# A fused matmul and batch norm on one core: work of VectorE moved to ScalarE and GpSimd, two output blocks turned another way, and the order of all work given as a table

## The chip, the cores and the metric

The kernel runs on one core of a Trainium2 chip. A core has five engines with instruction streams of their own: TensorE (PE) multiplies matrices, VectorE (DVE), ScalarE (ACT) and GpSimd (POOL) work on tiles, and SyncE (SP) issues transfers. Transfers run on 16 DMA engines, which all queues share; "the wire" is short for them. On-chip data lies in SBUF. TensorE writes into PSUM, of which there are eight banks here. The metric is the device time of one execution in microseconds, and the time before is the median of three runs.

## What is computed

```python
batch, m, k, n = 16, 512, 1024, 768
...
y = np.matmul(x, weight)
mean = np.mean(y, axis=(0, 1), keepdims=True)
var = np.var(y, axis=(0, 1), keepdims=True)
y_norm = (y - mean) / np.sqrt(var + eps)
return (gamma * y_norm + beta).astype(np.float32)
```

x is 8192 rows of 1024, the weight 1024 by 768, all float32. Mean and variance are taken per output column over all 8192 rows, so nothing of a column can be written before all its rows are multiplied. Products are made in bfloat16 and accumulated in float32. The output has 25.2 MB.

## The kernel before

**Tiles.** The rows are cut into 16 chunks of 512 (`C`, chunk `c`), the 768 columns into six tiles of 128 (`nt`). x is loaded chunk by chunk on GpSimd's queue until 100 us and turned by VectorE (L435). The first and second tile (`GA = 2`) are multiplied "by rows", x stationary, so that the result stands as it is stored (`rows_unit`, L510); only chunks 14 and 15 of them are multiplied "by columns" (`ga_unit`, L814) and turned later (`ga_block`). The third to sixth tile (nt 2 to 5) are multiplied "by columns", weight stationary (`col_unit`, L575), in halves of the contraction; a result then lies transposed and must be turned before it is stored. The third, fourth, fifth and sixth tile follow one another on TensorE.

**Statistics.** A result in PSUM is read twice: for its statistics and for a bfloat16 copy into SBUF ("keep"). On VectorE the statistics are one `bn_stats` (L711), with the keep on ScalarE (L715). For the tiles and chunks in `ASTAT` ScalarE does both, a keep with its sum (L720) and a square with its sum (L724); `total` (L978) then puts the sums together before the tile's variance is made. When a tile's chunks are done, variance, root and scale follow (`finish_tasks`).

**Output of the first two tiles** (`rows_out`). A block takes a product with the scale on VectorE (L937), an addition of the shift on GpSimd (L942) or, for the blocks in `ADDED`, on VectorE, and a store. The scale and shift rows are spread over the partitions by TensorE (`spread_rows`, L903); GpSimd has no access to PSUM in this kernel, and its shift row is copied to SBUF first (`shift_sbuf`).

**Output of the others.** A block has two chunks, 1024 rows. There are three ways:
- "pe": a norm (`norm`, L1021) on the columns, eight transposes on TensorE (`turn_block`), a copy from PSUM on ScalarE (L1210), a store (L1202). The eight transposes may ride inside a later matmul unit, one after each matmul ("hosted").
- "xact": the norm, a transpose by DMA on SP's queue (L1220), a conversion to float32 on ScalarE (L1232), a store.
- "raw" (`RAW`): the kept values are turned by DMA before the scale is known (`raw_turn`, L1106). The scale is then spread over rows (`raw_spread`: turn, gather, deal, keep), and the block takes a product on VectorE (L1174), an addition on GpSimd (L1178) and a store (L1182). Five blocks go this way.

**The tail.** The fifth tile's last block is held until the last matmul (`held_block`, L1252). The sixth tile's statistics are only complete then: aggregate, root (L1311), scale (L1324), and for each block norm (L1348), transposes (L1044), copy (L1361), store (L1364).

**Order.** Every step above is a `Task` with the engines that may run it, an estimate of its time, and a due time (`prio`). `arrange` plays the whole kernel through with those estimates. It picks the next task by due time among those that can begin within 0.2 us of the earliest. It also picks the engine where a task has several, places its buffers (PSUM banks through `Pool`, SBUF through `Space`), and decides which transposes ride in which matmul unit. The instructions are then issued to each engine in exactly the order that comes out (`seq`). On the chip an engine runs its own list in order and waits by semaphores for the others.

Of the kernel before, what the change touches and what calls it, by code (L numbers as in the profile page):

```python
# [120 lines left out]

def arrange(tasks, turns, log=None):
# [6 lines left out]
    left = sorted(tasks, key=lambda t: t.prio)  # L129
    order = []  # L130
    SEM, LOOK = 0.06, 0.2
# [36 lines left out]
    while left:  # L168
        seen = [(t, ready(t)) for t in left]
        first = {}  # L170
        for t, r in seen:
            if r is not None:
                for e in t.engines:
                    b = start_of(t, r, e)
                    if e not in first or b < first[e]:
                        first[e] = b
        if not first:
            raise RuntimeError(f"nothing can begin: {[(t.prio, t.emit) for t in left[:8]]}")
        e = min(first, key=lambda k: first[k])
        best = None  # L180
        for t, r in seen:
            if r is not None and e in t.engines and start_of(t, r, e) <= first[e] + max(LOOK, t.look):
                if best is None or t.prio < best[1]:
                    best = start_of(t, r, e), t.prio, t
        start, _, t = best
# [4 lines left out]
        if t.hosts:  # L190
            room = t.hosts
            for u, r in seen:
                if u in turns and r is not None and r <= start + 0.3 and room >= 1:
                    n = min(room, turns[u][0])
                    if turns[u][0] == turns[u][1]:
                        places = [s.pool.place(s) for s in u.takes]
                        if any(p is None or p[0] > start for p in places):
                            continue
                        for s in u.takes:
                            s.pool.take(s, s.pool.place(s)[1])  # L200
                        u.takes_done, u.takes = u.takes, []
                    t.hosted.append((u, n))
                    turns[u][0] -= n
                    room -= n
                    occ += 0.0555 * n
                    lat += 0.0555 * n
# [12 lines left out]
        left.remove(t)  # L219
        for u, n in t.hosted:  # L220
            if turns[u][0] == 0:
                u.end = t.end + 0.2
                left.remove(u)
# [4 lines left out]
def kernel(  # L228
# [136 lines left out]
    def act(occ):  # L365
        return {"ACT": (occ, occ + 0.11)}
# [549 lines left out]

    U = S - 30.0
# [9 lines left out]
    sh = task(U, act(0.3), shift_sbuf, [p1], uses=[a1_slot])  # L927


    def rows_out(c, s0, s1, k):  # L930
# [19 lines left out]
        a = task(due, dve(0.3 * n), norm, [p0] + keeps, takes=[slot], uses=[y_row[c], a0_slot])  # L950
# [5 lines left out]
    k = 0  # L956
# [6 lines left out]
    def negate_gamma(eng):  # L963
        seq(nc.vector.tensor_scalar(ngamma, gamma_sb, -1.0, None, op0=ALU.mult))

    ng = task(S, dve(0.1), negate_gamma, [affine, sr], True)

    def finish_tasks(nt):
# [41 lines left out]
        if nt in ASTAT:  # L1010
            deps = [task(now + 1.0, {"ACT": (1.2, 1.3)}, total, deps)]
# [44 lines left out]
    def ga_block(c, due):  # L1056
# [4 lines left out]
        def norm_ga(a):  # L1061
            def emit(eng):
                part = yslot.y[:, a]
# [348 lines left out]
```

## Time and profile before

| | |
|---|---|
| time, median of 3 runs (lowest to highest) | 206.29 us (206.23 to 206.86) |
| span of the profiled execution | 204.07 us |
| the median less that span | 2.22 us |
| TensorE, VectorE, ScalarE, GpSimd busy | 189.3, 159.3, 146.2, 124.1 us |
| last matmul of the sixth tile ends | 186.62 us |
| read from memory, written | 36.71 MB, 25.17 MB |

The span runs from the first to the last instruction of one execution under the profiler; no total time is known for that execution, so its span is set against the median of the runs. In the slices of the page the span is cut into 40 equal parts and a digit is the busy share in tenths. A line of the chain has a start, a length and the work that the end was waiting for. A line of a stage has the busy time of each engine, with the count of instructions in brackets. A line of waits has who waited for whom, and the total, the count and the longest in microseconds.

### The profile page before, as it was taken

Reading aid. Unit: us, or ns where it says so; the run is one execution under the profiler, and the core shown is the slowest. Engines: PE = TensorE matmul, PEld = TensorE weight load, DVE = VectorE, ACT = ScalarE, POOL = GpSimd, SP = SyncE. Lnnn points to the kernel's source line nnn. Section 1 sums busy time; section 2 is a strip of 40 time slices with the busy share of each in tenths; the row PEclk is TensorE's granted clock in tenths of the full one; section 3 lists DMA queues with packets and bytes.
Section 4 is the critical chain, followed back from the end, with each engine's and each line's share of the span. In section 5 each row is a group of like instructions: output and inputs, shape, how many; then the busy total and the mean of one; then the engine's idle time right before and its main releaser. Section 6 shows DMA issues by size and latency. Waiting matters only on the chain.

```text
span 204.1 us, 3510 instructions
## 1 busy us (share of the span) xinstructions
PE 189.3 (93%) x1210; PEld 114.5 (56%) x1210; DVE 159.3 (78%) x250; ACT 146.2 (72%) x260; POOL 124.1 (61%) x150
## 2 busy tenths in 40 slices
PE   7969999999999999999999999999999999997900
PEld 3457554657488888777865444444444445544600
DVE  4031879999999999969989998987999878657900
ACT  2001461368989999899978766999998959956950
POOL 7776954877499989997403999389613312940000
PEclk9999999999999999999999999999999999999965
DMA  4999999999999999999686899899999999999998
GB/s 71 172 199 196 176 196 196 196 197 197 190 193 197 197 196 196 196 197 195 103 181 200 297 339 336 248 301 328 295 322 227 336 303 274 347 343 310 310 347 253
DMA packets 98562, 48.74 MB, mean 239 GB/s; under 512 B 24304, under 2 KB 98032, under 8 KB 98544
## 3 DMA queue, kind: packets, MB, share of 16 engines
q0 software_dynamic: 34624, 18.36, 65.5%
q1 hardware_dynamic: 63920, 30.16, 52.6%
q8 instruction: 9, 0.15, 0.3%
q14 instruction: 9, 0.07, 0.1%
HBM read 36.71 MB, written 25.17 MB: 303 GB/s over the span
## 4 chain that ended last, share of the span: by engine, by line
PE 86%; ACT 3%; DMA 3%; POOL 2%; issue 1%; ACTq 0%; DVE 0%; POOLq 0%
PE y_ps L575 54%; PE y_ps L510 24%; PE y_ps L814 4%; ACT o_sb L1361 3%; DMA ring<-in_x_dram 3%; PE o_ps L1044 1%; POOL ring L403 1%; POOL w_sb L387 1%; PE y_ps L753 1%; PE a_ps L903 1%; PE o_ps L1074 0%; ACTq L1407 0%; PE idle_ps L591 0%; PE tot_ps L871 0%; ACT ring L1252 0%
## 5 line engine op out<-in xcount | busy, mean ns | idle before, releaser
L575 PEld LDWEIGHTS <-w_sb 128*128 128x128 bf16 x520 | 50.3, 97 | 57.6
L575 PE MATMUL y_ps<-xT_sb,w_sb 128*128 128x512 bf16 (+1 forms) x272 | 59.3, 371 | 0.0
L575 PE MATMUL y_ps<-x_pl,w_sb 128*128 128x512 bf16 x248 | 57.4, 379 | 0.0
L403 POOL DMA_DIRECT2D ring<-in_x_dram x76 | 47.2, 626 | 14.4 <-DMA ring<-in_x_dram 5.5
L510 PE MATMUL y_ps<-w_sb,xT_sb 128*128 128x256 bf16 x448 | 50.6, 273 | 1.7 <-DMA ring<-in_x_dram 1.6
L510 PEld LDWEIGHTS <-xT_sb 128*128 128x128 bf16 x448 | 43.5, 98 | 9.4 <-DVE xT_sb L435 2.9
L435 DVE STREAM_TRANSPOSE xT_sb<-ring 128x1024 f32<-128x1024 f32 (+1 forms) x29 | 31.2, 1111 | 14.1 <-DMA ring<-in_x_dram 13.9
L711 DVE BATCH_NORM_STATS2 stats<-y_ps 128x6 f32<-128x512 f32 x46 | 30.9, 687 | 7.7 <-PE y_ps L575 7.2
L715 ACT CAST y_sb<-y_ps 128x512 bf16<-128x512 f32 x51 | 29.0, 593 | 10.4 <-DVE stats L711 6.3
L547 ACT COPY x_pl<-xT_sb 128x1024 bf16<-128x1024 bf16 x32 | 32.8, 1063 | 1.7 <-DVE xT_sb L435 1.7
L942 POOL TENSOR_TENSOR ring<-ring,sum 128x1024 f32<-128x1024 f32 (+1 forms) x11 | 23.8, 2188 | 14.9 <-ACT y_ps L724 10.9
L659 ACT ACTIVATE sq_sb<-y_ps 128x512 f32<-128x512 f32 x28 | 16.3, 610 | 16.2 <-PE y_ps L510 15.9
L666 POOL TENSOR_TENSOR sum<-sum,sq_sb 128x512 f32<-128x512 f32 x20 | 25.6, 1278 | 3.0 <-ACT sq_sb L659 1.7
L662 DVE TENSOR_TENSOR sum<-y_ps,sum 128x512 f32<-128x512 f32 x28 | 18.9, 675 | 6.3 <-ACT sq_sb L659 5.3
L672 ACT CAST y_sb<-y_ps 128x512 bf16<-128x512 f32 x28 | 16.3, 594 | 8.2 <-DVE sum L662 8.0
L1178 POOL TENSOR_TENSOR ring<-ring,sum 128x1024 f32<-128x1024 f32 x6 | 14.8, 2477 | 9.8 <-issue 8.5
L937 DVE TENSOR_TENSOR ring<-y_sb,a_ps 128x1024 f32<-128x1024 bf16 (+1 forms) x16 | 16.7, 1079 | 0.1
L1044 PE MATMUL o_ps<-ident,y_sb 128*128 128x128 bf16 x104 | 13.1, 221 | 1.6 <-DVE y_sb L1348 1.5
L1232 ACT CAST ring<-ring 128x1024 f32<-128x1024 bf16 x13 | 13.8, 1063 | 0.6 <-DMA ring<-y_sb 0.6
L1145 POOL COPY sum<-sum 32x256 f32<-32x256 f32 (+1 forms) x17 | 5.8, 340 | 13.4 <-DVE sum L1142 6.5
L428 DVE STREAM_TRANSPOSE xT_sb<-ring 128x2048 bf16<-128x2048 bf16 x6 | 13.5, 2290 | 0.1
L591 PE MATMUL idle_ps<-idle_sb 128*128 128x512 f32 x18 | 9.6, 688 | 1.5 <-DVE idle_sb L316 1.5
(104 smaller groups left out, 153.7 us busy)
## 6 DMA issues: line engine op xcount, KB each, us to landing
out_dram<-ring SPq DMA_DIRECT2D x37, 512.0 KB, 3.4
ring<-in_x_dram POOLq DMA_DIRECT2D x52, 256.0 KB, 8.8
out_dram<-o_sb SPq DMA_DIRECT2D x6, 512.0 KB, 4.7
ring<-in_x_dram POOLq DMA_DIRECT2D x16, 128.0 KB, 5.9
w_sb<-in_weight_dram POOLq DMA_DIRECT2D x8, 192.0 KB, 6.2
out_dram<-ring SPq DMA_DIRECT2D x6, 256.0 KB, 3.0
ring<-in_x_dram POOLq DMA_DIRECT2D x4, 192.0 KB, 7.8
out_dram<-o_sb SPq DMA_DIRECT2D x3, 256.0 KB, 2.5
```

The source lines that it names most:

```text
L403: bi = seq(nc.gpsimd.dma_start(x_bf[32 * i:32 * i + 32], src[:, :, KQ * i:KQ * (i + 1)]))
L435: seq(nc.vector.transpose(dst, src[:, :, jw0:jw1]))
L510: seq(nc.tensor.matmul(y_ps[:, s], x_of(c, jw, e, t * P, (t + 1) * P), w_sb[:, jw, e, 0:NA], start=(s == 0 and jw == 0 and e == 0), stop=( ...
L547: seq(nc.scalar.copy(dst, pairs) if eng == "ACT" else ENG[eng].tensor_copy(dst, pairs))
L575: seq(nc.tensor.matmul(y_ps, w_sb[:, jw, e, nt * P:(nt + 1) * P], moving(c, jw, e, q0 * QR, q1 * QR, parted), start=(jw == 0 and e == 0 an ...
L659: seq(nc.scalar.activation(sq_sb[:, 0:n], slot.tile[:, 0:n], AF.Square))
L662: seq(nc.vector.tensor_add(sum1, slot.tile[:, 0:n], sum1))
L666: seq(ENG[eng].tensor_add(acc, acc, state["sq"][:, 0:n]))
L711: seq(nc.vector.bn_stats(dst, slot.tile))
L715: seq(nc.scalar.copy(y(nt, c), slot.tile))
L937: seq(nc.vector.tensor_mul(slot.o, y_row[c].y[:, s0:s1], aff[0][:, None, :].to_broadcast([P, n, NA])))
L942: seq(ENG[eng].tensor_add(slot.o, slot.o, row[:, None, :].to_broadcast([P, n, NA])))
```

## The change

1. `ORDER`, a table of 785 words, replaces the choice in `arrange`. A word is an engine's letter (P TensorE, V VectorE, A ScalarE, G GpSimd, S SP) and a task's number in order of creation; behind a plus sign stand the transposes that ride along, as block and count. `arrange` still places the buffers and plays the times through, in the table's order.
2. `RAW` of the fourth tile becomes `(0, 2)`: its block of chunks 2 and 3 goes the raw way, as the sixth raw block. It went the "xact" way.
3. `MODE` of the fifth tile: the block of chunks 8 and 9 goes the "xact" way. It went the "pe" way.
4. `ASTAT` gets the fourth tile's chunks 12 and 13. Their statistics are made on ScalarE, and `total` is done for that tile too; it now waits only for the chunks that it sums.
5. `SCALED = (2,)`: the product of the second half of chunk 0 in `rows_out` moves to GpSimd, which reads the scale row from a copy in SBUF that ScalarE makes (`scale_sbuf`).
6. `negate_gamma` moves from VectorE to GpSimd and doesn't wait for the first tiles' shift any more.
7. `norm_ga` of chunk 15 may run on ScalarE; in the table one of its two halves does.
8. `PAD` goes from 50 to 28. The tile `stats` gets 528 bytes shorter per partition; the two new tiles of `ASTAT` take 128 and 400.

Up to the end of x's loads, about 97 us, the table has the order of the kernel before on every engine. Behind that it differs on all of them. Some words of it: S664 is the DMA transpose of the fifth tile's chunks 8 and 9 and S575 that of the fourth tile's last block; P660, P668 and P672 are transposes of the fifth tile's blocks; P536 is the first half of the fourth tile's chunk 11 and A507 the keep of its chunk 15; A457 makes the third tile's scale; A727 is the last root, A733 and A736 the copies of the held block; V750, P751, A752 and S753 are norm, transposes, copy and store of the sixth tile's chunk 2, 512 rows. The fifth tile's "gather" is G647, on GpSimd; it ran on ScalarE.

```diff
+ORDER = (
+    "G0 P59 G3 G8 A9 G4 G7 V1 V2 P60 G10 P61 P62 P63 P64 P65 V5 V6 P66 G12 P67 P68 P69 P70 P71 G14 P76 A72 "
...
+    "V329 P421 P425 P330 P331 P422 A318 A332 A333 A389 V384 V334 V383 V335 V388 P385 P426 P390 A386 S393 S398 "
...
+    "S366 S369 V456 V371 V526 V373 V510 V502 A457 A468 A488 A472 A476 A494 S469 S372 S473 A503 A470 P504 P517 "
+    "P505 P496 V379 V506 V458 V518 A511 A480 A507 A474 A527 A484 A519 A495 G377 G374 G380 G459 G460 S378 S471 "
+    "S375 P610 P520 P536 P497 P537 P512 P513 P532 P533 P521 S477 S481 S381 S475 A498 A461 A478 V579 V580 V581 "
...
+    "A572 V645 V671 V659 V667 V677 V663 V685 V646 V681 A686 A641 A678 G647 P695+668.3 P691+660.4 P699+660.4 "
+    "P687 P688 P692+672.1,668.1 P700+668.1,672.1 P696+668.3,672.1 S569 S664 S575 G648 A661 A665 A682 A649 "
+    "A576 V693 V689 V650 V701 G651 A694 A669 A702 A690 S573 S662 S666 S577 P711+672.1 P707+672.3 P708 P712 "
+    "P719 P703+672.1 P704 P715 P716 V653 V656 V713 V697 V720 V709 V731 V705 V725 A673 A710 A714 A706 A698 "
+    "G654 G729 G657 P722 V717 V723 P735 P732 V726 V728 A718 A721 A727 A733 S670 S652 S655 S674 S658 V730 V750 "
+    "V754 V738 V746 V755 P751 P739 P747 A736 A724 A752 A740 A748 V742 V759 V780 V769 V784 V760 V774 V764 V770 "
...
+)
...
-    left = sorted(tasks, key=lambda t: t.prio)
+    left = tasks
...
+    NAMES = {"P": "PE", "V": "DVE", "A": "ACT", "G": "POOL", "S": "SP"}
+    for word in ORDER.split():
+        word, _, riders = word.partition("+")
+        t, e = left[int(word[1:])], NAMES[word[0]]
+        r = ready(t)
+        if r is None:
+            raise RuntimeError(f"out of order: {word}")
+        start = start_of(t, r, e)
...
-    PAD = 50
+    PAD = 28
...
-    ASTAT = {2:tuple(range(4,16))}
+    ASTAT = {2:tuple(range(4,16)),3:(12, 13)}
...
-    ADDED = (0,6,16,28,40)
+    ADDED, SCALED = (0,6,16,28,40), (2,)
...
-    MODE = {2:'xact',3:'xact',4:('pe',)*8}
+    MODE = {2:'xact',3:'xact',4:('pe','pe','pe','pe','xact','pe','pe','pe')}
...
-    RAW, RAWADD, RAWDUE = {2:(0,2),3:(0,),4:(0,2,4)}, {2:'POOL',3:'POOL',4:'POOL'}, {2:14.0,3:8.0,4:8.0}
+    RAW, RAWADD, RAWDUE = {2:(0, 2),3:(0, 2),4:(0, 2, 4)}, {2:'POOL',3:'POOL',4:'POOL'}, {2:14.0,3:8.0,4:8.0}
...
+    def scale_sbuf(eng):
+        seq(nc.scalar.copy(sum3[:, NA:2 * NA], aff[0]))
...
-            seq(nc.vector.tensor_mul(
-                slot.o, y_row[c].y[:, s0:s1], aff[0][:, None, :].to_broadcast([P, n, NA])))
+            row = sum3[:, NA:2 * NA] if eng == "POOL" else aff[0]
+            seq(ENG[eng].tensor_mul(slot.o, y_row[c].y[:, s0:s1], row[:, None, :].to_broadcast([P, n, NA])))
...
+        on = pool(0.59 * n) if k in SCALED else dve(0.3 * n)
...
-        seq(nc.vector.tensor_scalar(ngamma, gamma_sb, -1.0, None, op0=ALU.mult))
-
-    ng = task(S, dve(0.1), negate_gamma, [affine, sr], True)
+        seq(nc.gpsimd.tensor_scalar(ngamma, gamma_sb, -1.0, None, op0=ALU.mult))
+
+    ng = task(S, pool(0.3), negate_gamma, [affine])
...
-            deps = [task(now + 1.0, {"ACT": (1.2, 1.3)}, total, deps)]
+            deps = deps + [task(now + 1.0, {"ACT": (1.2, 1.3)}, total, [col_end[nt, c][0] for c in ASTAT[nt]])]
...
+                if eng == "ACT":
+                    seq(nc.scalar.activation(
+                        part, part, AF.Identity, bias=shift[:, a:a + 1], scale=scale[:, a:a + 1]))
+                    return
...
-        norms = [task(due, dve(0.25), norm_ga(a), [sr] + [h[1] for k, h in ga_half.items() if k[1] == c], True, uses=[yslot])
+        norms = [task(due, dve(0.25) if c == RC else {**dve(0.25), **act(0.48)}, norm_ga(a), [sr] + [h[1] for k, h in ga_half.items() if k[1] == c], True, uses=[yslot])
...
```

More of the change, by code (lines that the diff above doesn't have):

```diff
@@ L166, in start_of @@
         return b
[L168 to L185, printed above, removed]
+    NAMES = {"P": "PE", "V": "DVE", "A": "ACT", "G": "POOL", "S": "SP"}
[6 more added lines that the diff above has]
+        start = start_of(t, r, e)
         for s in t.takes:
@@ L189, in arrange @@
         t.hosted = []
[L190 to L206, printed above, removed]
+        for rider in riders.split(",") if riders else ():
+            i, n = rider.split(".")
+            u, n = left[int(i)], int(n)
+            if turns[u][0] == turns[u][1]:
+                for s in u.takes:
+                    s.pool.take(s, s.pool.place(s)[1])
+                u.takes_done, u.takes = u.takes, []
+            t.hosted.append((u, n))
+            turns[u][0] -= n
+            occ += 0.0555 * n
+            lat += 0.0555 * n
         if t in turns:
@@ L218, in arrange @@
         order.append(t)
-        left.remove(t)
         for u, n in t.hosted:
@@ L927 @@
     sh = task(U, act(0.3), shift_sbuf, [p1], uses=[a1_slot])
+    sh0 = task(U, act(0.3), scale_sbuf, [p0], uses=[a0_slot])
     def rows_out(c, s0, s1, k):
```

6 lines of the change are left out of this document (3 added, 3 removed), and 27 rows, old and new, of the table ORDER.

## The prediction

> **What bounds the kernel now.** I read the page's busy shares and slices first, then the chain that ended last, then the waits of TensorE, then busy time by stage, and last the DMA slices of the final 54 us.
>
> ```profile
> PE 189.3 (93%) x1210; PEld 114.5 (56%) x1210; DVE 159.3 (78%) x250; ACT 146.2 (72%) x260; POOL 124.1 (61%) x150
> PEclk9999999999999999999999999999999999999965
> DMA  4999999999999999999686899899999999999998
> ```
>
> ```profile
> 106.66 1.05 PE a_ps L903 x8
> ...
> 109.95 0.45 PE o_ps L1074 x8
> 110.40 58.94 PE y_ps L575 x269
> 169.34 0.06 PE o_ps L1044
> ...
> 177.82 6.99 PE y_ps L575 x32
> 184.80 1.81 PE y_ps L753 x16
> 186.62 0.24 PE o_ps L1044 x4
> ```
>
> ```profile
> PE o_ps L1044 <- DVE y_sb L1348: 1.5, 1, 1.5
> ```
>
> The chain (start, us, what) is TensorE without a break from 24 us to 186.6. In the list of TensorE's waits nothing lies between the start and the 1.5 us at 187, where the last tile's scale is awaited. The clock is full throughout. So until 186.62 the time is the sum of TensorE's instructions, whatever the other engines do, as long as none makes it wait.
>
> Behind 186.62 come 17.45 us of tail: 2.69 to the issue of the last tile's first store (189.31), then 4.19 MB of stores. The wire in that stretch (GB/s, slices of 1.35 us from 150 on):
>
> ```profile
> GB/s 314 327 326 312 152 131 348 305 346 342 232 329 347 294 318 324 150 347 348 347 347 346 340 342 347 346 346 341 210 293 268 345 346 347 348 346 347 346 331 1
> ```
>
> 346 is its ceiling. It is full from 173 to 188.8, drops to 210, 293, 268 until 192, then is full to the end: 4.19 MB at 346 GB/s are 12.1 us. The dip shows that the older stores have run out before the last tile's arrive. So the end is "last matmul, time to the first store of the last tile, 12.1 us of wire". Busy time by stage, for cover (stage, its length, then PE, PEld, DVE, ACT, POOL with counts, clock, DMA share, GB/s):
>
> ```profile
> 132.00:144.00 12.00, 12.00 (x57) 5.36 (x55) 9.93 (x15) 12.00 (x18) 11.19 (x12) 1.00 1.04 310
> 144.00:156.00 12.00, 12.00 (x58) 5.38 (x56) 11.76 (x27) 11.32 (x18) 4.64 (x8) 1.00 1.19 316
> 180.00:187.00 7.00, 7.00 (x47) 4.01 (x44) 3.93 (x9) 3.14 (x7) 2.05 (x1) 1.00 1.14 343
> ```
>
> ScalarE and VectorE have no room between 132 and 156 and plenty after 180.
>
> **The parts of the change.**
>
> Fifth tile, chunks 8 and 9, turned by DMA. TensorE loses 8 transposes; eight of them standing together took 0.45 us (L1074 above), and each takes 0.06 inside the stream. They lie on the path: **-0.45 us**. The ScalarE copy from PSUM (1.01, L1210) becomes a conversion in SBUF (1.06, L1232): nothing. SP gains one DMA transpose, 1.3 to 2.4 us (L1220).
>
> Sixth raw block (fourth tile, chunks 2 and 3). Its transpose moves from the full stretch near 155 to the five at 100 to 107 us, of 1.25 us each (L1106), where the wire carries nothing else; all six end near 108.3, before the first output store's issue at 109.1. VectorE: 1.21 (L1174) for 0.54 (L1026). ScalarE: no conversion, -1.06. GpSimd: +2.48 (L1178). With the first part, the DMA transposes in the full stretch stay at 14, so the wire's work there changes by 0; at worst +1.28 (one transpose), which the dip of 1.04 us would mostly take up.
>
> Statistics of the fourth tile's chunks 12 and 13 on ScalarE: VectorE -2 x 0.69 (L711); ScalarE's casts of 0.59 become pairs of 1.17 (L720, L724 with their reads, start to start), +1.16, and the summing adds 0.9 (L980 to L986, 123.25 to 124.15) between the last statistic and the root. That wait holds up the conversions and copies behind it on ScalarE, and the fourth tile's stores; not TensorE, unless banks run out (below).
>
> The table moves two of the sixteen re-layout copies (L547) from ScalarE (1.06) to VectorE (0.68), one rows-scaling of 0.68 (L937) from VectorE to GpSimd (at the add's 1.29, L942), one 0.41 (L1064) to ScalarE (between the 0.59 of L715 and half of L1023's 1.25), adds a 0.37 copy for the scale, moves four small copies of the fifth tile (1.0) from ScalarE to GpSimd, and a 0.16 negation likewise. Sums: VectorE -0.68 -0.41 -0.16 -1.38 +0.67 +1.36 = -0.6; ScalarE +0.6 +0.37 +1.16 +0.9 -1.06 -2.12 +0.05 -1.0 = -1.1; GpSimd +1.29 +0.2 +2.48 +0.9 = +4.9 of a span in which it idles 80. All covered by TensorE's stream: 0. Without that cover, VectorE and ScalarE would return 0.6 and 1.1.
>
> One row speaks against leaning on GpSimd: a VectorE copy of L547 at 143.1 took 0.96 where the median is 0.68, and a raw add was running (141.1 to 146.3). The new 4.9 us can meet about as many copies and norms as two raw adds do, at most four: 4 x 0.28 = 1.1 us, covered. The Trainium skill (SBUF — State Buffer, "Who interferes with whom") has a two-port VectorE copy and a GpSimd instruction block each other fully. By that, the sum for VectorE would be four waits of up to a whole raw add; by the row it is four of 0.28, and the trace, with no copy above 0.96, agrees with the page on the contact and not on its size.
>
> The spread of the first tiles' scale. In the table the first and second tile's scale is spread (L903) behind only 4.3 us of other TensorE work after the sums, against 7.1 now. TensorE now idles 0.09, 0.07 and 0.05 there. The chain's last input ends about 0.9 earlier too. I take **-0.1**, between -0.2 (the idle gone) and 0.
>
> Banks. The table leaves half-finished units open and statistics waiting. I walked the tightest place by rows. When chunk 11 of the fourth tile begins, eight PSUM banks are held (chunks 9, 8, 6, 12, 15, 13, 7 and an opened fifth-tile one); it needs chunk 15's. TensorE arrives at 136.8: the third tile ends at 122.8 (the spreads' end, 107.7, plus 15.1 of halves), then 9 halves of 0.86 and 7 of 0.9. ScalarE starts the third tile's scale at 126.45, as now, and has 0.79, five norms of 1.15, one statistic of 0.6, three casts of 0.48 and one conversion of 0.95 before the bank is free: 136.0. Slack some 0.7 us, where the kernel now shows no such wait: **0**, with an open upper end.
>
> Tail. The table puts the root ahead of both held copies (it started 0.04 after its input anyway: 0) and makes a 512-row block the first of the last tile instead of a 256-row one. Its norm costs 0.06 more (0.405 against 0.342), two more transposes 0.11, its copy 0.24 (0.616 against 0.376): the first store goes out 0.41 later. It brings 256 KB instead of 128, so the two gaps of the first small stores close: they are issued 0.47 and 0.51 apart and fill the wire for 0.38 each, 0.22 together. **+0.2**, between -0.2 (the delay hidden behind held stores still on the wire) and +0.4.
>
> Sum: -0.45 -0.1 +0.2 = -0.35. The profiled execution spans 204.07; the median of the runs is 206.29, 2.22 above it, which I keep: 203.72 + 2.22 = **205.9 us**.
>
> **Rivals.**
> - The tail comes out early (faster): TensorE's saving arrives whole, the idle at 106 goes and the first store isn't late. -0.45 -0.2 -0.2: 205.4. For it: the wire dips by 1.04 us there, so anything sooner counts. Against: the larger first block. Chance 0.31.
> - ScalarE late, banks run out (slower). Place: 125 to 137, from the inversion of the third tile's deviation to chunk 15's cast. Now that inversion ends 0.9 us after its root, behind a 1.2 us product. Two norms' worth of lateness, 2.3, less the slack of 0.7, stalls TensorE 1.6: 207.5. It decides from a lateness of 1.7 (a stall of 1.0). Against: no such stall now. Chance 0.22.
> - VectorE blocked outright by GpSimd (slower): two blocks of a whole 2.48 between 132 and 156, where VectorE has 2.3 idle of 24, would leave 2.7 us and stop TensorE for about that: 208.6. The largest seen is 0.28, so 0.06. This is the page's rule named above.
> - The wire sets the end, and TensorE's saving is hidden (no change). The fourth tile's last DMA transpose stands behind the fifth tile's new one on SP, which waits for that tile's scale (166.2 now), three norms and a statistic ahead of its own norm (4 x 0.54 + 0.69) and then takes 1.7: issued near 170.7, two microseconds later than the 168.7 now. If older stores still fill the wire when the first last-tile store comes, the saving is gone: one transpose of 1.28 less the dip of 1.04, 206.5. Chance 0.06. The Trainium skill (Advanced Engine Details and Errata, "X-Bar Transpose (TRN2)") has transposes as fast as ordinary transfers; five of 256 KB in 6.86 us (the timeline, L1106) are 191 GB/s against 346, so the trace disagrees.
>
> **How the numbers follow.** The forecast, 0.35, has its own range from its bounds, 205.4 to 206.2. I call within 0.3% of the median "same" (205.67 to 206.91), about what a measurement can tell. Faster 0.31, from the first rival; same 0.35 + 0.06 = 0.41; slower 0.22 + 0.06 = 0.28. The range 205.2 to 207.6 goes down to the early tail and up to the bank rival, and leaves out the outright block, the longer stalls and a tail better than any row shows.
>
> **What would show it.** Right: TensorE unbroken to 186.0 to 186.2, 24 hosted transposes, six transposes at 100 to 108.3, first last-tile store about 3.1 us after the last matmul, a smaller or equal dip on the wire. Wrong: TensorE waiting on ScalarE or VectorE between 120 and 175 (banks); L547 copies on VectorE near 2 us (outright block); a full wire from 186 to the end (wire). A gain over 1.1 us would mean a saving that I don't see, since nothing else in the chain moves.

## The result and the profile after

The changed kernel takes 209.75 us (median of 6 runs, 208.97 to 210.35). The kernel before, run beside it, takes 206.12 (205.84 to 206.86). The ratio is 1.017, with a 95% interval of 1.0144 to 1.0197: the change costs 3.6 us. I had predicted 205.9 us and a range of 205.2 to 207.6.

The profiled execution took 210.35 us and spans 208.56. First the page of the changed kernel, with its busy shares, the slices of TensorE's clock, and the wire in GB/s (40 slices of 5.2 us):

```profile
PE 190.3 (91%) x1202; PEld 115.4 (55%) x1202; DVE 161.6 (77%) x248; ACT 144.9 (69%) x267; POOL 131.1 (63%) x157
PEclk9999999999999999999999999999999999999695
GB/s 75 159 196 191 169 196 196 196 197 197 190 194 196 197 197 195 196 197 193 99 121 114 381 385 333 279 346 297 317 249 252 264 325 326 348 322 227 313 347 226
```

TensorE's clock is full up to the last matmul, as it was before. Then TensorE's waits in it (who waits for whom; total, times, longest), of which the kernel before had only the load's, the start's and 1.5 us of the last-tile line:

```profile
PE o_ps L1074 <- DVE y_sb L1382: 3.1, 3, 2.7
PE y_ps L534 <- DMA ring<-in_x_dram: 1.7, 1, 1.7
PE idle_ps L615 <- DVE idle_sb L340: 1.5, 1, 1.5
PE o_ps L1108 <- DVE y_sb L1098: 1.3, 1, 1.3
PE y_ps L599 <- ACT y_sb L739: 0.2, 1, 0.2
```

And its chain (start, length, what). Before, it was TensorE without a break from 24 us to 186.6. Now it is on TensorE from 80.9 on, leaves it from 108.7 to 110.8, then from 142.5 to 174.0, where it runs over GpSimd, ScalarE and above all VectorE, and from 183.7 on until the last tile's scale is made. The first and the last of these:

```profile
107.62 1.07 PE a_ps L927 x8
108.99 0.37 ACT sum L942
109.39 0.69 DVE ring L966
110.08 0.68 DVE y_sb L1098
110.80 0.62 PE o_ps L1108 x8
...
181.75 1.96 PE y_ps L599 x9
183.73 1.30 DVE stats L735 x2
...
185.96 2.17 DVE y_sb L1056
188.13 0.61 DVE stats L735
...
190.88 0.32 ACT std L1345
```

Near its end stands a norm of VectorE (L1056) of 2.17 us on the chain, 2.25 in all. The same norm took 0.51 to 0.63 everywhere in the kernel before.

A span can be cut into four stretches: up to the first real matmul; from there to the last matmul ("stream"); from there to the issue of the last tile's first store; and the rest. All in us, from the profiled executions:

| kernel | start | stream | to first last-tile store | rest | span |
|---|---|---|---|---|---|
| before | 12.14 | 174.48 | 2.69 | 14.76 | 204.07 |
| changed | 12.74 | 176.36 | 4.18 | 15.28 | 208.56 |
| difference | +0.60 | +1.88 | +1.49 | +0.52 | +4.49 |

The start is chance: other runs of kernels with this table start between 11.71 and 12.32, and the profiled run lies 0.60 above its own median. Of the stream's 1.88, the wait at 109 is 1.43 (from start to start of TensorE's instructions). Two waits at 171.5 and 173.6, for a norm of the fifth tile and for a keep on ScalarE (L739), are 0.23 and 0.37. Waits for the loads at 80 and 98 are 0.33 and 0.14, against 0.22 at 25.6 before; they differ from run to run in every kernel here. The eight transposes saved are -0.45. That adds up to 1.83. Of the tail's 1.49, the root comes 1.78 after the last matmul instead of 0.79 (+0.99), and the first store 2.40 after the root instead of 1.90 (+0.49). Of the rest's 0.52, 0.43 lies behind the landing of the last store (shown below, at the fifth tile's block). Without the start and the waits for loads, which are 0.25 longer, the two profiles differ by 3.64, as the medians do.

### The profile page after: what moved, and what is told of

It reads as the page before. It is cut to its first block, busy times and chain, and to the rows that moved or that the text cites. A ratio compares the mean times of both kernels' runs of the same rounds, so it can differ in the third digit from the quotient of the medians.

```text
span 208.6 us, 3505 instructions
## 1 busy us (share of the span) xinstructions
PE 190.3 (91%) x1202; PEld 115.4 (55%) x1202; DVE 161.6 (77%) x248; ACT 144.9 (69%) x267; POOL 131.1 (63%) x157
## 4 chain that ended last, share of the span: by engine, by line
PE 34%; DVE 24%; DMA 18%; issue 8%; ACT 7%; POOL 4%; ACTq 1%; DVEq 0%; POOLq 0%
PE y_ps L599 23%; DMA ring<-in_x_dram 12%; DMA w_sb<-in_weight_dram 6%; DVE stats L735 6%; PE y_ps L534 5%; PE y_ps L838 4%; DVE xT_sb L459 3%; DVE y_sb L1056 3%; POOL ring L427 3%; ACT y_sb L739 2%; DVE x_pl L571 2%; DVE xT_sb L452 2%; DVE sum L686 2%; ACT o_sb L1395 2%; DVE y_sb L1382 1%
## 5 line engine op out<-in xcount | busy, mean ns | idle before, releaser
L599 PE MATMUL y_ps<-xT_sb,w_sb 128*128 128x512 bf16 (+1 forms) x272 | 60.2, 371 | 0.0
L739 ACT CAST y_sb<-y_ps 128x512 bf16<-128x512 f32 x49 | 27.2, 588 | 8.7 <-DVE stats L735 3.4
L571 ACT COPY x_pl<-xT_sb 128x1024 bf16<-128x1024 bf16 x30 | 30.6, 1058 | 3.1 <-DVE xT_sb L459 1.7
L690 POOL TENSOR_TENSOR sum<-sum,sq_sb 128x512 f32<-128x512 f32 x20 | 25.6, 1280 | 2.8 <-ACT sq_sb L683 2.1
L1212 POOL TENSOR_TENSOR ring<-ring,sum 128x1024 f32<-128x1024 f32 x7 | 17.2, 2475 | 9.7 <-DVE ring L1208 4.3
L735 DVE BATCH_NORM_STATS2 stats<-y_ps 128x6 f32<-128x512 f32 x30 | 19.3, 680 | 4.1 <-PE y_ps L599 4.1
L696 ACT CAST y_sb<-y_ps 128x512 bf16<-128x512 f32 x28 | 16.3, 593 | 8.3 <-DVE sum L686 8.0
L966 DVE TENSOR_TENSOR ring<-y_sb,a_ps 128x1024 f32<-128x1024 bf16 (+1 forms) x15 | 16.1, 1106 | 3.9 <-DMA out_dram<-ring 2.7
L1179 POOL COPY sum<-sum 32x64 f32<-32x64 f32 (+1 forms) x21 | 8.9, 426 | 12.4 <-DVE sum L1176 11.6
L1074 PE MATMUL o_ps<-ident,y_sb 128*128 128x128 bf16 x96 | 11.6, 247 | 3.2 <-DVE y_sb L1382 3.1
L735 DVE BATCH_NORM_STATS2 sums<-y_ps 128x6 f32<-128x512 f32 x18 | 11.8, 680 | 1.1 <-PE y_ps L599 1.1
```

The costliest lines, as they stand in the source:

```text
L571: seq(nc.scalar.copy(dst, pairs) if eng == "ACT" else ENG[eng].tensor_copy(dst, pairs))
L599: seq(nc.tensor.matmul(y_ps, w_sb[:, jw, e, nt * P:(nt + 1) * P], moving(c, jw, e, q0 * QR, q1 * QR, parted), start=(jw == 0 and e == 0 an ...
L690: seq(ENG[eng].tensor_add(acc, acc, state["sq"][:, 0:n]))
L735: seq(nc.vector.bn_stats(dst, slot.tile))
L739: seq(nc.scalar.copy(y(nt, c), slot.tile))
L1212: seq(ENG[eng].tensor_add(slot.o, slot.o, row[:, None, :].to_broadcast([P, n, P])))
```

## The experiments

All times are medians, each beside the kernel before on the same chip in the same session (medians there 205.94 to 206.09). Ratios are to that.

### Which waits cost: three moves in the table, alone and together

Theory A: the wait at 109 costs its full length. Theory B: the long norm at 185.9 is blocked by a GpSimd add and delays the root. Rival C: the late stores cost. In the changed kernel the first store goes out at 113.54 (109.10 before), because two of the six raw transposes on SP's queue wait until 111.8 for SBUF that the first products free. On the timeline (SP's issues: start, length, what):

```profile
100.96 12.26 SPq L1140 DMA_TRANSPOSE r_sb<-y_sb  x6
113.54 0.40 SPq L974 DMA_DIRECT2D out_dram<-ring  x1
```

**A, the norm first.**

```diff
-    "... A389 V384 V334 V383 V335 V388 P385 P426 P390 A386 S393 S398 "
+    "... A389 V384 V383 V334 V335 V388 P385 P426 P390 A386 S393 S398 "
```

> Edit to the changed kernel: one word of the table moves. VectorE's norm of chunk 14 (V383) goes ahead of the first product (V334). In the changed kernel the product waited 1.15 us for ScalarE's copy of the scale, the norm stood behind it, and TensorE stopped 1.43 us at 109.2 for that norm. Theory A (the stall is real time, since TensorE's stream sets the end): the stall goes and the time falls by 1.2 to 1.5 us. Rival (VectorE, ScalarE or the wire are the bound further on and give the stall back): the stall goes and the time falls by less than 0.5 us, with new or longer waits of TensorE after 140.

Measured: 209.09 us, ratio 1.0146 (1.0119 to 1.0172), 0.5 to 0.7 below the changed kernel, with intervals that overlap. TensorE's wait did not go. It moved by one norm, to that of chunk 15 (V388), which still stood behind product and addition, and shrank from 1.43 to 0.95. VectorE's timeline in this run (start, length, line; in brackets the idle time ahead and what ended it):

```profile
106.49 0.73 DVE L1098 TENSOR_SCALAR y_sb<-y_sb,scale,shift 128x512 bf16<-128x512 bf16 x2
108.05 0.69 DVE L966 TENSOR_TENSOR ring<-y_sb,a_ps 128x512 f32<-128x512 bf16 x1 [0.83 <-ACT sum L942]
109.22 0.69 DVE L970 TENSOR_TENSOR ring<-ring,a_ps 128x512 f32<-128x512 f32 x1 [0.48 <-DVE ring L966]
109.83 0.41 DVE L1098 TENSOR_SCALAR y_sb<-y_sb,scale,shift 128x512 bf16<-128x512 bf16 x1
```

The 0.48 that came off the wait is about what the time fell by, but this run alone does not show the fall clear of the noise; the kernel with all the moves, below, does. The expected 1.2 to 1.5 was wrong for this edit. The bracket of the product is the origin of the whole: it waits for ScalarE's copy of the scale (L942), which the change added. The product's line in the kernel before and in the changed kernel:

```profile
107.59 0.68 DVE L937 TENSOR_TENSOR ring<-y_sb,a_ps 128x512 f32<-128x512 bf16 x1
```

```profile
109.39 0.69 DVE L966 TENSOR_TENSOR ring<-y_sb,a_ps 128x512 f32<-128x512 bf16 x1 [1.15 <-ACT sum L942]
```

In the instruction records the first product waits for TensorE alone before the change, and for TensorE and ScalarE after it. Both read the same PSUM tile, and the later reader in the order of issue is made to wait.

**B, the held block's norm to VectorE's idle stretch.**

```diff
-    "... V685 V646 V681 A686 A641 A678 G647 ..."
+    "... V685 V646 V681 A686 A641 V731 A678 G647 ..."
...
-    "... V653 V656 V713 V697 V720 V709 V731 V705 V725 A673 ..."
+    "... V653 V656 V713 V697 V720 V709 V705 V725 A673 ..."
```

> Edit to the changed kernel: the norm of the fifth tile's held block (V731) moves on VectorE from 185.9, where a GpSimd add of 2.36 us began 0.4 us ahead of it and it took 2.25 us, to about 175, where VectorE idles and GpSimd runs small copies only. Theory B (VectorE's two-port norm is blocked outright until GpSimd's add ends): the norm takes 0.5 to 0.6 us there, the last root comes 1.3 to 1.7 us earlier after the last matmul, and the time falls by 1.0 to 1.6 us. Rival (VectorE's backlog of statistics and products holds the root up anyway): less than 0.5 us.

Measured: 208.23 us, ratio 1.0105 (1.0084 to 1.0126), 1.3 to 1.5 faster than the changed kernel. The norm takes 0.55 there, at 173.3, and the root comes 0.79 after the last matmul, exactly as before the change (1.78 in the changed kernel). B holds. In the changed kernel the two engines stood like this (GpSimd's add, VectorE's norm):

```profile
185.48 2.37 POOL L1212 TENSOR_TENSOR ring<-ring,sum 128x1024 f32<-128x1024 f32 x1
```

```profile
185.87 2.25 DVE L1056 TENSOR_SCALAR y_sb<-y_sb,scale,shift 128x1024 bf16<-128x1024 bf16 x1
```

The norm begins 0.39 after the add and ends 0.29 after the add's end: it stood still until GpSimd was done.

**C, the first stores ahead of the waiting transposes.**

```diff
-    "S395 S394 S336 S387 G337 ..."
+    "S336 S387 S395 S394 G337 ..."
```

> Edit to the changed kernel: on SP's queue the first two stores go ahead of the fifth and sixth raw transpose, which wait until 111.8 us for SBUF that the first products free. The first store, at 113.5 us now and at 109.1 before the change, is issued near 111.4. Theory A and B (the wire has slack at the end): no change, within 0.4 us. Rival C (late stores free ring pieces late, so the first raw add waits 2.4 us for a store at 145.7 and then blocks a copy of VectorE at 149): faster by 0.5 to 1.5 us, and the add at 145.7 starts earlier.

Measured: 210.25 us, ratio 1.0203 (1.0175 to 1.0230), 0.5 to 0.7 slower, with intervals that overlap. The first store went out at 110.93, 2.6 us sooner, but TensorE got a new wait of 0.68 at 136.75, for a bank, which is as long as the time lost. The raw add did not start earlier (145.97 for 145.73). So C found no support: no gain shows from the earlier stores, and the wire of the changed kernel runs nearly dry at 191 anyway.

**All three, and ScalarE copies the scale ahead of the shift** (`A333 A332`).

> Edits to the changed kernel: the three above at once, and ScalarE copies the scale ahead of the shift. If A and B are right and add up: faster than the changed kernel by 2.3 to 3.1 us, so 206.6 to 207.4 and still not below the kernel before, since TensorE's waits of 0.6 at 171 to 174 stay. If the losses hide one another: 1.5 us or less.

Measured: 207.19 us, ratio 1.0058 (1.0036 to 1.0079). As expected: 2.3 to 2.6 us of the loss are gone. No wait at 109 is left; one of 0.59 for a bank has come at 134.6, and the two at 169 to 172 (0.24 and 0.36) remain. Against B alone this kernel is 1.0 us faster, and the two intervals don't meet. The 1.43 at 109 less the new 0.59 is 0.84. So the wait at 109 was real time: A holds.

### What remains: more waits taken away

**Three waits.** To the moves of A and B: chunk 15's norm goes ahead of the product as well, the scale's copy ahead of the shift's, and the fifth tile's norms stand in the order in which TensorE wants them. The stores keep their place.

```diff
-    "... A318 A332 A333 A389 V384 V334 V383 V335 V388 P385 ..."
+    "... A318 A333 A332 A389 V384 V383 V388 V334 V335 P385 ..."
...
-    "A572 V645 V671 V659 V667 V677 ..."
+    "A572 V645 V667 V659 V671 V677 ..."
```

> Edits to the changed kernel: on VectorE both norms of chunk 14 and that of chunk 15 go ahead of the first product; ScalarE copies the scale ahead of the shift; the held block's norm goes to VectorE's idle stretch at 175; the fifth tile's norm of chunks 10 and 11, which TensorE wants first, and that of 6 and 7 go ahead of that of 12 and 13, which waits 1.0 us for a copy of ScalarE. The stores keep the place that they have in the changed kernel. Theory (the losses are five misplaced words of the table, one after another on the path): no wait of TensorE at 109, 135 or 171, at most 0.4 us at 173; 206.1 to 206.7, level with the kernel before. Rival (the parts themselves load VectorE and ScalarE too much): the waits return elsewhere and the time stays at 207 or above.

Measured: 207.00 us, ratio 1.0055 (1.0036 to 1.0074), above the 206.1 to 206.7 of the theory. Apart from the start and the last tile, one wait of TensorE is left:

```profile
PE y_ps L599 <- DVE ring L966: 0.5, 1, 0.5
```

It is at 134.5 and 0.67 long by TensorE's starts. The last product of the first tiles waits 2.65 for a store that holds its ring piece, and until it is done it holds the bank of the scale, which TensorE needs. The wait for the fifth tile's norms is gone, and yet the time equals that of the kernel with all three.

**The transposes behind the ninth store.** The same, with `S395 S394` behind `S342`.

> The five moves of the kernel with three waits mended, and on SP's queue the fifth and sixth raw transpose behind the ninth store instead of ahead of the first. In the mended kernel the first store went out at 111.9 (109.1 before the change), the last product of the first tiles waited 2.65 us for a store to free its ring piece, and TensorE waited 0.67 at 134.5 for the bank of the scale that this product still read. If that chain is right: first store near 109, no TensorE wait of more than 0.2 at 134, time 0.5 to 0.9 below the mended kernel, 206.1 to 206.5. If TensorE's wait has another cause: it stays, and the time is 206.8 to 207.2.

Measured: 207.15 us, ratio 1.0050 (1.0038 to 1.0063). The wait at 134.5 is gone, so the chain was right. The time did not fall to the expected 206.1 to 206.5.

**A 256-row block first in the tail.** To that, `V738`, `P739`, `A740` and `S741` go ahead of the 512-row block's.

> The mended kernel with the raw transposes behind the ninth store, and in the tail a 256-row block of the last tile ahead of the 512-row one (norm, transposes, copy, store). If the larger first block costs what the tail's sum says: the first last-tile store 0.3 to 0.5 us sooner behind the last matmul than 3.65, and the time 0.2 to 0.5 below 207.15. If the wire then has gaps between the small stores: the time unchanged.

Measured: 207.08 us, ratio 1.0064 (1.0050 to 1.0079). The first last-tile store comes 3.13 after the last matmul instead of 3.65, so the block's size is 0.5 of the way to the first store. The time is unchanged.

In these three kernels VectorE's scale (L1358) also begins 0.41 us after the semaphore in front of it is passed, against 0.06 in the changed kernel, and no event in the trace explains it. They stay 1.0 to 1.3 us above the kernel before. By the stretches, 0.4 to 1.0 of that is a later first store of the last tile, 0.2 to 0.6 a longer rest, in which the end behind the last landing alone is 0.43 longer (see the fifth tile's block below), and 0.2 to 0.6 a longer stream, in which the saved 0.45 does not show; the profiled starts differ by -0.4 to +0.2. Which waits lengthen the stream was followed up only as far as told above. No version of the table tried here beats the kernel before. Another contact of a copy with an add, at 149 (below), was left as it is, and what it costs was not tested.

### The parts without the table

**All the parts, order chosen by due times as before.**

> The changed kernel with all its parts, but without the table: the order is again chosen as in the kernel before, by due times. If the table's order is what costs: 205.4 to 206.6, with no TensorE wait between 100 and 186. If the parts cost (a sixth raw block without SBUF for its transpose, more GpSimd adds to block VectorE): 207.5 or more, with copies or norms of VectorE above 1.5 us.

Measured: 207.54 us, ratio 1.0077 (1.0054 to 1.0101). So the table as it stands costs about 2 us more than the old way of choosing, and the parts cost about 1.6 by themselves: each theory has a share. TensorE waits 0.70 at 110, for a norm that stood opposite a GpSimd add (1.32 for 0.41 at 109.5), and 1.07 at 170, for a norm of the usual 0.53. The chain to that one goes back over VectorE's statistics, a conversion on ScalarE (1.05 at 167.8) and a norm blocked by a GpSimd add (1.59 for 0.53 at 162.4) to a product that waited 1.9 for a store.

**One part alone: the fifth tile's block by DMA.**

```diff
-    MODE = {2:'xact',3:'xact',4:('pe',)*8}
+    MODE = {2:'xact',3:'xact',4:('pe','pe','pe','pe','xact','pe','pe','pe')}
```

> The kernel before with one part alone, the fifth tile's chunks 8 and 9 turned by DMA; the order is chosen as before. By my sum: eight transposes less on the path, 0.45 us faster, 205.4 to 205.9. Rival (the transpose by DMA goes into a full wire and pushes the last stores): 206.0 to 206.8.

Measured: 207.14 us, ratio 1.0058 (1.0036 to 1.0079), above both cases. The stream is 174.15, 0.33 shorter than before, so TensorE's saving is there. But the rest is 16.91 instead of 14.76. The dip in the wire from 188 to 192 is gone, and at the end a trickle goes on. Windows of this run (stretch, its length, then the engines' busy times, clock, DMA share, GB/s):

```profile
186.00:192.00 6.00, 4.44 (x54) 3.02 (x53) 5.22 (x19) 5.16 (x11) 0.00 (x0) 1.00 1.15 346
...
202.00:203.00 1.00, 0.00 (x0) 0.00 (x0) 0.00 (x0) 0.00 (x0) 0.00 (x0) 0.50 0.91 274
203.00:204.00 1.00, 0.00 (x0) 0.00 (x0) 0.00 (x0) 0.00 (x0) 0.00 (x0) 0.50 0.10 31
204.00:205.00 1.00, 0.00 (x0) 0.00 (x0) 0.00 (x0) 0.00 (x0) 0.00 (x0) 0.50 0.03 8
```

**Is it the wire?** First try: two stores of the fourth tile cut to an eighth.

```diff
-            seq(ENG[eng].dma_start(dst(), slot.o))
+            few = slice(0, 1 if nt == 3 and c in (8, 10) else count)
+            seq(ENG[eng].dma_start(dst()[:, few], slot.o[:, few]))
```

> The kernel before with the fifth tile's chunks 8 and 9 turned by DMA, and two stores of the fourth tile (chunks 8 to 11) cut to an eighth, so that 0.92 MB less goes over the wire (2.65 us at 346 GB/s); those rows of the output are not written. If the wire sets the end of the kernel with that part alone (207.14, full wire from 175 to the end): 205.3 to 205.9, since TensorE's 0.45 then shows. If something else adds its 1.2 us: no change, 206.8 or more.

> The kernel before with the same two stores cut to an eighth; those rows of the output are not written. By the prediction's view (the end is the last matmul, the time to the first store of the last tile, and 12.1 us of wire; older stores have run out by then): 0 to 0.5 us faster, 205.5 to 206.0. If the wire bounds the kernel before too: 1.5 to 2.6 us faster.

Measured: 207.20 us, ratio 1.0050 (1.0038 to 1.0062), and 206.02, ratio 0.9997 (0.9986 to 1.0009). The first told nothing: with the cut the wire fell to 131 and 162 GB/s at 170 to 174, so what was taken away lay ahead of an idle stretch. From 176 on it was full again (344). So the cut was made behind that stretch, at the three raw stores of the fifth tile:

```diff
-            m0 = c * CH
+            m0, few = c * CH, 1 if nt == 4 else n
             seq(nc.sync.dma_start(
-                out_flat[m0:m0 + n * P, nt * P:(nt + 1) * P].rearrange("(s p) n -> p s n", p=P), slot.o))
+                out_flat[m0:m0 + few * P, nt * P:(nt + 1) * P].rearrange("(s p) n -> p s n", p=P), slot.o[:, 0:few]))
```

> The kernel before with the fifth tile's chunks 8 and 9 turned by DMA, and the three stores of the fifth tile's raw blocks cut to an eighth. They are issued between 176 and 186, behind the last stretch in which the wire ran empty, where the first cut (stores issued before 172) may have changed nothing because the wire went idle after it. 1.38 MB less, 4.0 us at 346 GB/s; those rows are not written. If the wire's backlog from 175 on sets the end: 205.3 to 205.8, and the wire has a dip before the last tile's stores. If not: 206.8 or more.

> The kernel before with the same three stores cut to an eighth; those rows are not written. If the wire has run out of older stores by 189 there, as its dip says: 0 to 0.4 us faster, 205.6 to 206.1. If the wire bounds the kernel before as well: 1 us or more faster.

Measured: 205.78 us, ratio 0.9998 (0.9984 to 1.0013), with the DMA block, and 205.76, ratio 0.9989 (0.9977 to 1.0000), without it. With the DMA block the cut gives 1.2 to 1.4 us, without it 0.2. So with that part alone the wire's backlog sets the end, and in the kernel before it does not, as the prediction read from the dip. The 0.45 of TensorE does not show even then; the two are equal within their intervals.

The traces show where it goes. With the DMA block and this cut the stream is 0.32 shorter than with the cut alone (174.34 against 174.66). But from the landing of the last store to the end of the span it takes 1.35 us instead of 0.92. SP's last instructions wait for eight semaphores, always in the same order, and each takes 0.06 us even if its store landed long ago. SP's DMA instructions signal these eight in turn. The kernel before has 88 of them on SP, so the last store signals the eighth semaphore, and SP goes on at once. With the DMA block there are 89, the last store signals the first one, and seven more follow: 0.43 us. All 18 traces fit: 0.91 to 0.93 us from the landing to the end in the six with 88 DMA instructions on SP, 1.34 to 1.35 in the twelve with 89, all kernels with the table among them. So the DMA transpose costs at the very end about what its eight transposes save on TensorE. No run changed the number of DMA instructions and nothing else. Of the 2.15 by which the rest is longer with this part alone, 0.43 is this, and about 1.5 is the trickle.

**One part alone: the sixth raw block** (`3:(0,)` becomes `3:(0, 2)` in `RAW`).

> The kernel before with one part alone, the sixth raw block; the order is chosen as before. If its transpose fits with the five ahead of the first store: 206.0 to 206.4. If it waits for SBUF that the first products free, as in the changed kernel, and SP's queue with it: the first store later than 109.5 by 1 to 4 us, and the time 0 to 1 us longer; if its added GpSimd work blocks VectorE in the stretch 132 to 156, a copy or norm above 1.5 us and a time above 207.

Measured: 208.04 us, ratio 1.0091 (1.0067 to 1.0115). Neither case as I had put them: the six transposes are issued by 108.5, the first store is at 109.62, no copy or norm is longer than 0.75, the stream is 174.93, and TensorE never waits in it behind 26. The rest is 16.77. The wire in this run falls to 172 GB/s in the slice from 170 to 175 (SP stands in front of a store until 173.2, waiting 2.7 us for ScalarE), and is nearly full from there on:

```profile
GB/s 73 157 200 196 194 196 196 196 197 196 190 194 197 196 198 194 196 197 193 92 188 258 317 340 260 281 335 298 308 339 187 327 333 172 319 345 347 343 347 153
```

That the lost wire time comes back as backlog at the end is what the rows suggest; it was not tested for this part.

**The small moves alone** (statistics of chunks 12 and 13, `SCALED`, the negation, the norm of chunk 15, `PAD`; neither raw nor DMA block).

> The kernel before with the small moves alone (statistics of the fourth tile's chunks 12 and 13 on ScalarE, one product and the negation on GpSimd, the norm of chunk 15 allowed on ScalarE, the smaller pad) and neither the sixth raw block nor the fifth tile's block by DMA; order chosen as before. By my sum these are covered: 205.8 to 206.3. If they cost by themselves (ScalarE late before the fourth tile's root, a first product that waits for ScalarE's copy of the scale): TensorE waits at 110 or in 125 to 137, and 206.8 or more.

Measured: 207.25 us, ratio 1.0052 (1.0040 to 1.0064). TensorE waits 0.70 at 110.1, for the norm of chunk 15. GpSimd in this run, and TensorE:

```profile
108.14 1.17 POOL L942 TENSOR_TENSOR ring<-y_sb,sum 128x512 f32<-128x512 bf16 x1 [8.16 <-ACT sum L918]
109.38 1.28 POOL L946 TENSOR_TENSOR ring<-ring,sum 128x512 f32<-128x512 f32 x1
```

```profile
110.11 0.22 PE L1084 MATMUL o_ps<-ident,y_sb 128*128 128x128 bf16 x1
110.86 0.56 PE L1084 MATMUL o_ps<-ident,y_sb 128*128 128x128 bf16 x7 [0.53 <-DVE y_sb L1074]
```

The product that was moved to GpSimd lets its addition follow at 109.38, and the norm on VectorE, begun at 109.49, took 1.32 instead of 0.41. That is 0.70 of the 1.16 lost. In the profile the rest is also 0.43 longer than before (15.19 us), for a cause that was not found.

**The same without the GpSimd product** (`SCALED = ()`; the expectation calls the addition at 109.38 the product).

> The small moves alone, but the product of chunk 0's second half stays on VectorE. With the small moves (207.25) GpSimd ran that product from 109.38 to 110.66, VectorE's norm of chunk 15 stood opposite from 109.49 and took 1.32 us instead of 0.41, and TensorE waited 0.70 at 110.1. If that contact is the cost: the norm takes 0.41, TensorE's wait is gone, and the time falls by 0.5 to 0.8, 206.4 to 206.8. If the wait comes from VectorE's load (which now has one product of 0.69 more): the wait stays and the time is 207.0 or more.

Measured: 209.49 us, ratio 1.0179 (1.0166 to 1.0192). Both cases miss. The norm took 0.41 and the wait at 110 shrank to 0.2, so the contact was that wait's cause. But the rule that chooses the order then put a raw product ahead of the last tile's last statistics (186.18, the root 1.86 after the last matmul), and the time rose by 2.2. In the profile the first last-tile store comes 1.4 later behind the last matmul than with the product on GpSimd, and the rest is 1.4 longer (16.62 us). With an order that is chosen anew, "one part alone" measures the part and a new order together. That holds for every kernel of this section whose order was chosen anew; only what their traces show is safe.

## Why the prediction was wrong

The forecast was 3.85 us too low. The profiles put this at six places: the wait at 109 (1.43), the saving at the spread that did not come (0.1), the waits at 171.5 and 173.6 (0.60), the late root (0.99), the first store beyond the 0.2 that I had booked (0.29), and SP's end (0.43).

**Eight transposes less: -0.45.** Right for TensorE. It has 1202 matmul instructions for 1210, and the stream of the DMA part alone is 0.33 shorter, with the usual spread in the waits for loads. But the term failed as a gain of the whole kernel: I put the DMA transpose that takes their place at nothing, and as the 89th DMA instruction on SP it lengthens the end by 0.43.

**"All covered by TensorE's stream: 0".** This step failed, at the first tiles' scale. I booked the copy of the scale as 0.37 of ScalarE's time and looked only at where it runs. What counts is who waits for it: the first product on VectorE. I had the row of the table, `V384 V334 V383`, in the diff, and did not ask what stands behind that product and who waits for it: the norm V383, and TensorE. Price: 1.43 of wait where the sum had -0.1 for the spread. Of these, 0.34 are a contact: the norm at 109.99 stood opposite the product that the change moved to GpSimd, and took 0.75 instead of 0.41.

**"Four waits of 0.28, covered".** This step failed, by a misread row. The copy of 0.96 at 143.1 was not a slight contact. It and the two adds opposite stand like this in the kernel before:

```profile
143.11 0.96 DVE L547 COPY x_pl<-xT_sb 128x1024 bf16<-128x1024 bf16 x1
```

```profile
141.10 5.19 POOL L1178 TENSOR_TENSOR ring<-ring,sum 128x1024 f32<-128x1024 f32 x2
```

The first of the two adds ended at 143.52, 0.41 after the copy began, and the copy ended 0.55 after that. It was an outright block that happened to be short. I should have set the row's excess against what was left of the add, not against the add's length. In the changed kernel VectorE loses 5.7 us in five contacts (0.12, 0.34, 1.71, 1.72, and 1.79 by a copy of 32 columns at 137.5), where I had booked 1.1. The rival "VectorE blocked outright", with 0.06, had the mechanism right for 0.99 in the tail and 0.34 at 109, but its place wrong: it had 132 to 156. A block of 1.71 did take place there, at 149 (2.39 for 0.68, the sign that I had named). TensorE did not wait beside it, but the copy lies on the chain that comes back to TensorE only at 174.0, behind the waits of 0.23 and 0.37. In the kernel with three waits mended the same block stays and these waits are gone, so there it was covered. In the tail nothing covers VectorE, and I had looked at 132 to 156 alone. By the Trainium skill (SBUF — State Buffer, "Who interferes with whom") the two engines hold a shared port pair one at a time for a whole instruction; the trace agrees (2.25 for 0.53 at 185.87), and the Trainium skill was better than my reading of the row.

**"All six end near 108.3, before the first output store's issue".** Wrong in the table's placement: two waited for SBUF until 111.8, and the first store was 4.4 late. No cost of it could be measured there (C). With the order chosen by due times the six are issued by 108.5 (sixth raw block alone).

**Banks, ScalarE late: 207.5 with 0.22.** Not in the changed kernel, where no wait of TensorE lies between 112 and 171. (136.84 less 135.98, the times as summed there, is a slack of 0.86, not 0.7.) In the mended kernels a bank was missing at 134, for another reason: a store that held a product's ring piece.

**Tail +0.2.** The larger first block delays the first store by 0.49, where I had 0.41; without the blocked norm the first store comes 3.17 after the last matmul (B), where I had 3.1. What of it reaches the end is less: with a small block first the time is the same. The root's delay of 0.99 is the block above.

**The wire, 206.5 with 0.06.** Not in the changed kernel: its wire falls to 18 GB/s in the window from 191 to 192, while the last tile is awaited. It is what happens to the DMA block when it comes alone (207.14), and there I had it too small, without the trickle and SP's end.

The range was too low above all because the sum took an engine's idle share as cover at two places without any: right behind the first tiles' scale, and behind the last statistics.

## What to carry to other kernels

When a step is added or moved, list who waits for it and what is queued behind the waiter, first at the places where one tile's scale releases everything and in the tail; a busy share gives no cover there. A VectorE copy or norm that meets a GpSimd add cost what was left of the add, less 0.1 to 0.3, so place such pairs by time and not by load. Look also at what follows the last landing: one DMA instruction more on SP cost 0.43 us there. With an order written out by hand, each word can be such a wait: reading the table against the timeline of the engine that ends last finds them, and here five moved words gave back 2.3 to 2.6 us, one of them 1.3 to 1.5 by itself.

## What the runs showed of the hardware

The block between VectorE and GpSimd is regular to a few hundredths. Eight VectorE instructions that began while a GpSimd add or product ran, from the records of the runs:

| kernel, instruction | begins | took (alone) | GpSimd's ends | ends after that |
|---|---|---|---|---|
| before, copy of 1024 columns | 143.11 | 0.96 (0.68) | 143.52 | 0.55 |
| changed, copy | 147.85 | 0.80 (0.68) | 148.10 | 0.55 |
| changed, copy | 149.03 | 2.39 (0.68) | 150.87 | 0.55 |
| parts without the table, copy | 139.56 | 1.23 (0.68) | 140.24 | 0.55 |
| changed, norm of 1024 | 185.87 | 2.25 (0.53) | 187.84 | 0.29 |
| parts without the table, norm | 162.39 | 1.59 (0.53) | 163.70 | 0.29 |
| changed, norm of 512 | 109.99 | 0.75 (0.41) | 110.59 | 0.15 |
| small moves, norm of 512 | 109.49 | 1.32 (0.41) | 110.66 | 0.15 |

The profile shows no wait for this: the blocked time counts as the instruction's own. In the other direction, an add of 128x1024, 2.34 to 2.43 alone, that begins under a VectorE copy or norm of 1024 columns takes up to 2.83, and ends 2.21 to 2.24 after the VectorE instruction does. VectorE's products with a PSUM operand, and its statistics from PSUM, show nothing of it: products of 1024 columns take 1.20 to 1.22 opposite adds in every trace.

The other thing is the end of the wire. In the DMA part alone and in the sixth raw block alone, a few packets at a time, and at the last one, go on for about 1.5 us when all the others are done (31 and 8 GB/s in the windows above). The DMA part with the first cut and the small moves without the GpSimd product end in the same way. In these four traces the wire never falls below 290 GB/s, by the microsecond, from 186 on; in the other fourteen, the kernel before with its dip at 188 to 192 among them, it does, and the transfers end nearly together. The last packets move 21 GB/s, a sixteenth of 346. That one of the 16 DMA engines carries a delay, which only an idle stretch of the wire lets it make up, would fit; the trace does not name the engine, and it stays open.
